# First feed-forward products with tokens in rows, transposed in 32x32 blocks by VectorE and put in place by DMA

## The chip, the cores and the metric

The kernel runs on one NeuronCore of one Trainium2 chip. The metric is the device time of one execution in microseconds (us); lower is better. A core has TensorE (PE, the matrix engine), VectorE (DVE), ScalarE (ACT), GpSimd (POOL), SyncE (SP, which here only issues transfers), and 16 DMA engines. Every engine takes its own instructions strictly in the order in which the program emits them; engines wait for each other by semaphores. On TensorE a matrix product is two instructions: a weight load (PEld, the stationary operand, at most 128x128) and the matmul that streams the moving operand past it into PSUM.

## The reference

Two layers over 256 tokens of width 2048, all in fp32. Each layer has a projection into a conv mixer, an HGRN2 mixer and a retention mixer, an output product, a layer norm, and a feed-forward block with squared ReLU:

```python
for l in range(DEPTH):
    proj = jnp.einsum('btd,de->bte', x, w_in[l])
    ...
    h = jnp.einsum('bte,ed->btd', mix, w_out[l])
    x = layer_norm(DEEPNORM_ALPHA * x + h, ln1_g[l], ln1_b[l]).astype(dtype)
    f = jnp.square(jax.nn.relu(jnp.einsum('btd,df->btf', x, w_ff1[l])))
    h = jnp.einsum('btf,fd->btd', f, w_ff2[l])
    x = layer_norm(DEEPNORM_ALPHA * x + h, ln2_g[l], ln2_b[l]).astype(dtype)
```

`w_ff1` is 2048 x 8192 and `w_ff2` 8192 x 2048. The change concerns the line with `f`: it must end as `f` transposed (columns of `f` on partitions, tokens along the row), since the second product contracts over the columns of `f`.

## The kernel before

**Precision.** TensorE multiplies numbers of a shortened fp32 format (fp32r). Every operand is therefore split into a high part (a rounded copy, made by a cast on ScalarE) and a low part (the rest, a subtraction on VectorE), and each product is the sum of three: high by high, high by low, low by high. For weights this is done in `unit` (L272): 512 KB of a loaded block become one unit, with the cast at L289 and the subtraction at L292. For activations it is `split_act` (L388), cast L391 and subtraction L393.

**Buffers.** Tiles come from rings: three `raw` buffers of 1 MB for loaded weights, six `wp` buffers for split units, eight `act` buffers (each four blocks of 128 contraction rows by 256 tokens, high and low), two `pair` buffers of 128 x 2048, eleven `r2` tiles of 128 x 512, four PSUM tiles `mm` for the large products and four `aux` for the small ones.

**Two forms of product.** `xstat` (L323) makes a group of 512 output columns with the tokens stationary: for each of 16 blocks of contraction and each of two halves of the tokens three matmuls at L315 of 512 columns, 96 in all. Its results are rows: tokens on partitions, columns of the output along the row. `wstat` (L349) makes 256 output columns with the weights stationary and the tokens moving: for each half of 128 columns and each of 16 blocks one matmul of 512 columns (L366: high weights by high and low tokens at once) and one of 256 (L368: low weights by high tokens), 64 in all. Its results are columns: output columns on partitions, tokens along the row. They leave PSUM by a copy on ScalarE (L375) and an addition on VectorE (L378). Both forms load weights by `load2` (L263), 1 MB for two units, issued from SyncE.

**Feed-forward.** For each of four chunks (`for c in range(NCH)`, L1063) four `act` buffers `fT` are filled with 2048 columns of `f`, transposed and split: eight calls of `wstat` (L1077), each followed by ReLU and square in one VectorE operation (L1079) and by `split_act` (L1082). Then four calls of `xstat` with `fT` as the stationary operand (L1099) make this chunk's part of the second product, added to the residual `x_nat` (L963). The very first 512 columns of a layer are an exception: they are made by `xstat` (L1074, so that the tokens whose norm is ready first can be used first: `head=HEAD`), squared in rows (`square_t`, L1066) and turned by TensorE: `transpose4` (L397) makes four 128x128 transposes against an identity matrix, and `split_act` takes them out of PSUM. `w1x` holds these columns' weights, `w1` those of the other 7680.

**Order.** A planner (`Plan`, L71) holds all operations with a cost for each and their dependences through buffers. `run` (L128) goes through them in the order of their planned start on each engine and emits them; among those that can start within 0.12 us it takes the one of least slack. The large products keep the program's order (`main`, L121), the preparation of a unit carries the product that needs it (`needed`, L301), other operations a fixed slack (`slack`, `floor`). Transfers are operations of an engine "DMA" whose results count as seen 2.0 us after their planned end; all of them are issued from SyncE's queue, in planned order. Waits in the running kernel come from the data dependences, whatever the plan assumed.

Of the kernel before, what the change touches and what calls it, by code (L numbers as in the profile page):

```python
# [17 lines left out]
P = 128  # L18
# [182 lines left out]
def block_kernel(ctx: ExitStack, tc: tile.TileContext, a: dict, out: bass.AP):  # L201
# [24 lines left out]
    def act(n, ptr=0, ps=False):  # L226
        return 0.000833 * n + (0.051 if ps else 0.093) + 0.093 * ptr

    def dve(n, ptr=0, fast=False):
        return (0.00052 if fast else 0.001042) * n + 0.069 + 0.06 * ptr  # L230
# [157 lines left out]
    def split_act(x, blks, cols, src, r, part, n=W, ps=False, **kw):  # L388

        nb = blks.stop - blks.start  # L390
        op("ACT", act(n, ps=ps), lambda: S.copy(out=x.t[:, 0, blks, cols], in_=bl(src(), nb)),  # L391
           r=r, w=[(x, part)], **kw)
        op("DVE", dve(n), lambda: V.tensor_tensor(out=x.t[:, 1, blks, cols], in0=bl(src(), nb),  # L393
                                                  in1=x.t[:, 0, blks, cols].bitcast(F32), op=ALU.subtract),
           r=r, w=[(x, part)], **kw)

    def transpose4(src, r, **kw):  # L397
        pt = aux.buf()

        def fn():  # L400
            for i in range(4):
                nc.tensor.transpose(out=pt.t[:, i * P:(i + 1) * P], in_=src()[:, i * P:(i + 1) * P], identity=ident)  # L402

        op("PE", 0.44, fn, r=r, w=[pt], **kw)
        return pt
# [566 lines left out]
        op("DVE", dve(W), fn, r=[ps], w=[(x_nat, (t, c))], **kw)  # L972


    norm = None
    for l in range(DEPTH):
        mixT = [acts.buf() for _ in range(4)]
        vt = []

        def vgroup(g, **kw):  # L980
            tl = []
            vt.append(tl)

            def done(t, ps):
                v = r2.buf()
                op("ACT", act(W, ps=True), lambda: S.copy(out=v.t, in_=ps.t), r=[ps], w=[v], floor=1.5)
                tl.append(v)

            xstat(a["wv"][l, g], xT, done, **kw)

        if l == 0:
            def before(i):
                first_x(i)
                if i == 3:
                    setup((plan.last["PE"],))

            vgroup(0, before=before, fine={0: 4, 2: 2, 4: 2, 6: 2})
            whole(xT[0])
        else:
            vgroup(0, head=HEAD)  # L1000
            norm.rest()
        pairs, gates = {}, {}
        for i, (kind, p) in enumerate(ORDER):
            if (kind, p) == ("hf", 2):
                vgroup(1)
            if (kind, p) == ("rq", 0):
                vgroup(2)
            if kind in ("hf", "rq"):
                pair = pairbufs.buf()
                pairs[kind[0], p] = pair  # L1010
            dst = None
            if kind in ("rq", "rk"):
                dst = (pairs["r", p], "Q" if kind == "rq" else "K", pv(pairs["r", p], 0 if kind == "rq" else 1))
            pr = wstat(a["wp"][l, i], xT, dst)
            if l == 0 and i == 1:
                op("DMA", 6.0, lambda: nc.sync.dma_start(out=x_nat.t, in_=a["x"].rearrange("(t p) d -> p t d", p=P)),
                   w=[x_nat], after=(plan.last["PE"],))
            if kind == "hf":
                hgrn_gates(l, p, pr, pair)
            elif kind == "hq":  # L1020
                Qv = pv(pair, 2)
                op("ACT", act(W), lambda Qv=Qv, pr=pr: S.activation(out=Qv(), in_=pr.t, func=AF.Sigmoid), r=[pr],
                   w=[(pair, "Q")])
                op("DVE", dve(W), lambda Qv=Qv, pr=pr: V.tensor_tensor(out=Qv(), in0=pr.t, in1=Qv(), op=ALU.mult),
                   r=[pr], w=[(pair, "Q")])
            elif kind == "hg":
                gate = r2.buf()
                op("ACT", act(W), lambda gate=gate, pr=pr: S.activation(out=gate.t, in_=pr.t, func=AF.Sigmoid),
                   r=[pr], w=[gate])
                hgrn(l, p, pairs["h", p], gate, vt, mixT)  # L1030
            elif kind in ("cg", "ca"):
                def uv(p=p):
                    return u_t.t[:, 2 * p:2 * p + 2, CONVW - 1:]

                uk = [(u_t, 2 * p), (u_t, 2 * p + 1)]
                if kind == "cg":
                    op("ACT", act(W), lambda uv=uv, pr=pr: S.activation(out=uv(), in_=bl(pr.t, 2), func=AF.Sigmoid),
                       r=[pr], w=uk)
                else:
                    op("DVE", dve(W), lambda uv=uv, pr=pr: V.tensor_tensor(out=uv(), in0=bl(pr.t, 2), in1=uv(),  # L1040
                                                                           op=ALU.mult), r=[pr], w=uk)
                    if p == 0:
                        accs = [r2.buf(), r2.buf()]
                    conv_taps(l, accs[p], 2 * p)
                    if p == 1:
                        conv(l, accs, mixT)
            elif kind == "rg":
                gate = r2.buf()
                op("ACT", act(W), lambda gate=gate, pr=pr: S.activation(out=gate.t, in_=pr.t, func=AF.Sigmoid),
                   r=[pr], w=[gate])  # L1050
                op("DVE", dve(W), lambda gate=gate, pr=pr: V.tensor_tensor(out=gate.t, in0=pr.t, in1=gate.t,
                                                                           op=ALU.mult), r=[pr], w=[gate])
                ret(l, p, pairs["r", p], gate, vt, mixT)
        for g in range(4):
            if g == 1:
                norm = Norm(a["l1g"][l], a["l1b"][l], 2 * l, True)
                norm.add(0, 0, held[0])
                norm.add(0, 1, held[1])
            held = {}
            xstat(a["wo"][l, g], mixT, (lambda t, ps: held.__setitem__(t, ps)) if g == 0 else  # L1060
                  (lambda t, ps: norm.add(g, t, ps)), tail=TAIL if g == 3 else 0)
        xT = norm.xT
        for c in range(NCH):  # L1063
            fT = [acts.buf() for _ in range(4)]

            def square_t(t, ps):  # L1066
                r = r2.buf()
                op("ACT", act(W, ps=True), lambda: S.activation(out=r.t, in_=ps.t, func=AF.Relu), r=[ps], w=[r])
                op("DVE", dve(W), lambda: V.tensor_tensor(out=r.t, in0=r.t, in1=r.t, op=ALU.mult), w=[r])
                pt = transpose4(lambda: r.t, [r, cst])  # L1070
                split_act(fT[0], slice(0, 4), slice(t * P, (t + 1) * P), lambda: pt.t, [pt], t, ps=True)

            if c == 0:
                xstat(a["w1x"][l], xT, square_t, head=HEAD)  # L1074
                norm.rest()
            for q in range(2 if c == 0 else 0, 8):
                r = wstat(a["w1"][l, 8 * c + q - 2], xT)  # L1077
                f = r2.buf()
                op("DVE", dve(W), lambda f=f, r=r: V.scalar_tensor_tensor(  # L1079
                    out=f.t, in0=r.t, scalar=0.0, in1=r.t, op0=ALU.max, op1=ALU.mult), r=[r], w=[f], floor=1.5)  # L1080
                o = (2 * q) % 4
                split_act(fT[q // 2], slice(o, o + 2), slice(0, T), lambda f=f: f.t, [f], ("o", o), floor=1.5)  # L1082
            lastc = c == NCH - 1
            for g in range(4):
                if lastc and g == 1:
                    norm = Norm(a["l2g"][l], a["l2b"][l], 2 * l + 1, False, l == DEPTH - 1)
                    norm.add(0, 0, held[0])
                    norm.add(0, 1, held[1])
                held = {}

                def add(t, ps, g=g, c=c):
                    if lastc and g == 0:
                        held[t] = ps
                    elif lastc:
                        norm.add(g, t, ps)
                    else:
                        residual(g, t, ps, c == 0, floor=1.5)

                xstat(a["w2"][l, c, g], fT, add, tail=TAIL if lastc and g == 3 else 0)  # L1099
        xT = norm.xT  # L1100
# [44 lines left out]
def _xs(w):  # L1145

    k, n = w.shape
    return w.reshape(k // 512, 2, 2, P, n // W, W)\
        .transpose(4, 0, 3, 1, 2, 5).reshape(n // W, k // 512, P, 2048)


def _ws(w):

    k, n = w.shape
    return w.reshape(2, 8, P, n // 256, 2, P).transpose(3, 4, 2, 0, 1, 5).reshape(n // 256, 2, P, 2048)
# [52 lines left out]
```

## Time and profile before

| | us |
|---|---|
| median of 3 runs | 2325.21 |
| lowest and highest run | 2323.97, 2325.35 |
| the profiled execution, its own time | 2324.98 |
| its span, first to last instruction | 2323.1 |

The profile shows one execution. "Busy" is the time in which an engine executes; waits, branches and the issuing of transfers don't count. The page's second part cuts the span into 40 slices, one digit for each (9 is 90% or more):

```profile
PE   9999999999999999999999999999999999999998
DVE  6999666765565565565679986657655655655655
ACT  6445444454344344344444554544444444444442
DMA  8544556465555555556554545564655555555563
```

The repeated patterns are the two layers. DMA moves

```profile
DMA packets 67706, 439.90 MB, mean 189 GB/s; under 512 B 7665, under 2 KB 7921, under 8 KB 16625
```

in the whole span. Five kinds of views are used below: the page; groups of instructions by source line, with count, total and mean duration, and the idle time ahead of them with what ended it; the chain of work that ended last, followed back from the last instruction; sums by windows of time; and the waits, who waited for whom, SyncE's queue (SPq) among them. Of a line's or a tile's own instructions a further view gives least, median and longest duration. Windows are given in us from the start of the span.

### The profile page before, as it was taken

How to read it: one execution, taken by the hardware profiler on the slowest of the kernel's cores; microseconds unless marked ns; L12 is line 12 of the kernel's file. 1: busy time of each engine (PE TensorE's matmuls, PEld its weight loads, DVE VectorE, ACT ScalarE, POOL GpSimd, SP SyncE). 2: the span in 40 equal slices, each digit the busy share in tenths (PEclk: the TensorE clock that was granted, in tenths of full speed). 3: DMA queues.
4: the chain of work that ended last, by engine and by line, in shares of the span. 5: the costliest groups of instructions: out<-in, count | busy, mean ns of one | idle time of the engine just before them, and what ended most of it. 6: DMA issues, size and time to landing. Idle time of an engine off the chain costs nothing.

```text
span 2323.1 us, 29492 instructions
## 1 busy us (share of the span) xinstructions
PE 2308.4 (99%) x11995; PEld 1961.7 (84%) x11995; DVE 1512.1 (65%) x2077; ACT 1055.0 (45%) x1346; POOL 47.1 (2%) x60
## 2 busy tenths in 40 slices
PE   9999999999999999999999999999999999999998
PEld 7888888888888888888888888888888888888886
DVE  6999666765565565565679986657655655655655
ACT  6445444454344344344444554544444444444442
POOL 0001000000000000000000000100000000000000
PEclk9999999999999999999999999999999999999999
DMA  8544556465555555556554545564655555555563
GB/s 297 186 166 164 174 195 209 165 211 195 193 188 185 196 184 197 188 189 203 209 173 164 175 165 179 179 227 166 205 192 189 185 196 189 192 185 196 183 232 112
DMA packets 67706, 439.90 MB, mean 189 GB/s; under 512 B 7665, under 2 KB 7921, under 8 KB 16625
## 3 DMA queue, kind: packets, MB, share of 16 engines
q1 hardware_dynamic: 67568, 438.01, 55.1%
q8 instruction: 94, 1.54, 0.3%
q14 instruction: 44, 0.35, 0.0%
HBM read 432.74 MB, written 2.10 MB: 187 GB/s over the span
## 4 chain that ended last, share of the span: by engine, by line
PE 98%; DMA 1%; ACT 1%; DVE 1%; issue 0%; SPq 0%; DVEq 0%; ACTq 0%
PE mm L315 44%; PE mm L366 34%; PE mm L368 17%; PE aux L634 1%; PE aux L402 1%; DMA raw<-in_wv 0%; ACT act L391 0%; DMA raw<-in_xt 0%; DVE wp L292 0%; PE aux L556 0%; PE aux L558 0%; PE aux L554 0%; PE aux L747 0%; ACT wp L289 0%; PE aux L610 0%; ACT r L943 0%
## 5 line engine op out<-in xcount | busy, mean ns | idle before, releaser
L292 DVE TENSOR_TENSOR wp<-raw,wp 128x1024 fp32r<-128x1024 f32 (+1 forms) x786 | 957.5, 1221 | 573.7 <-ACT wp L289 572.6
L366 PE MATMUL mm<-act,wp 128*128 128x512 f32 x3328 | 1180.3, 399 | 0.0
L289 ACT CAST wp<-raw 128x1024 fp32r<-128x1024 f32 (+1 forms) x786 | 824.8, 1052 | 770.9 <-PE mm L315 503.5
L315 PE MATMUL mm<-wp,act 128*128 128x512 f32 x4416 | 1017.8, 390 | 3.3 <-DVE wp L292 2.0
L315 PEld LDWEIGHTS mm<-wp,act 128*128 128x128 f32 x4416 | 824.5, 188 | 178.3 <-DVE wp L292 5.9
L368 PE MATMUL mm<-act,wp 128*128 128x256 f32 x3328 | 933.4, 280 | 0.0
L366 PEld LDWEIGHTS mm<-act,wp 128*128 128x128 f32 x3328 | 625.4, 188 | 151.9
L368 PEld LDWEIGHTS mm<-act,wp 128*128 128x128 f32 x3328 | 628.4, 189 | 0.7
L375 ACT COPY r<-mm 128x256 f32<-128x256 f32 x208 | 77.5, 373 | 368.2 <-PE mm L368 367.9
L378 DVE TENSOR_TENSOR r<-mm,r 128x256 f32<-128x256 f32 x184 | 78.0, 424 | 142.9 <-ACT r L375 142.2
L821 DVE SCALAR_TENSOR_TENSOR r<-u_t,cst,r 128x256 f32<-128x256 f32 x240 | 103.9, 480 | 0.0
L410 POOL TENSOR_TENSOR sm<-sm,mhalf 128x4 f32<-128x4 f32 (+1 forms) x24 | 28.6, 1193 | 2266.5 <-DVE sm L903 1611.8
L391 ACT CAST act<-r 128x512 fp32r<-128x512 f32 x82 | 51.4, 630 | 17.0 <-DVE r L1079 16.1
L393 DVE TENSOR_TENSOR act<-r,act 128x512 fp32r<-128x512 f32 x82 | 56.2, 685 | 0.0
L315 PE MATMUL mm<-act,act 128*128 128x512 f32 x192 | 44.8, 389 | 0.0
L970 DVE TENSOR_TENSOR x_nat<-x_nat,mm 128x512 f32<-128x512 f32 x48 | 31.1, 682 | 18.8 <-PE mm L315 18.7
L1079 DVE SCALAR_TENSOR_TENSOR r<-r 128x512 f32<-128x512 f32 x60 | 41.6, 693 | 2.1
L315 PEld LDWEIGHTS mm<-act,act 128*128 128x128 f32 x192 | 36.0, 188 | 7.5
L634 PEld LDWEIGHTS aux<-pair 128*126 128x126 f32 (+5 forms) x288 | 31.3, 173 | 3.9 <-DVE r L821 1.2
L634 PE MATMUL aux<-pair 128*126 128x64 f32 (+5 forms) x288 | 31.9, 253 | 0.0
L968 DVE SCALAR_TENSOR_TENSOR x_nat<-x_nat,mm 128x512 f32<-128x512 f32 x32 | 20.8, 682 | 13.1 <-PE mm L315 13.0
L923 ACT ACTIVATE x_nat<-x_nat,sm 128x512 f32<-128x512 f32 x6 | 4.9, 817 | 48.1 <-POOL sm L416 48.1
(123 smaller groups left out, 591.5 us busy)
## 6 DMA issues: line engine op xcount, KB each, us to landing
raw<-in_w SPq DMA_DIRECT2D x248, 1024.0 KB, 4.8
raw<-in_wp SPq DMA_DIRECT2D x88, 1024.0 KB, 4.8
raw<-in_wo SPq DMA_DIRECT2D x32, 1024.0 KB, 4.8
raw<-in_wv SPq DMA_DIRECT2D x20, 1024.0 KB, 4.8
raw<-in_w1x SPq DMA_DIRECT2D x8, 1024.0 KB, 5.2
raw<-in_wv SPq DMA_DIRECT2D x6, 512.0 KB, 6.0
pair<-pair SPq DMA_DIRECT2D x24, 128.0 KB, 2.3
x_nat<-in_x SPq DMA_DIRECT2D x1, 2048.0 KB, 9.4
```

Source lines behind the costliest of these rows:

```text
L289: S.copy(out=wt()[:, 0, sl], in_=raw.t[:, rs])
L292: V.tensor_tensor(out=wt()[:, 1, sl], in0=raw.t[:, rs], in1=wt()[:, 0, sl].bitcast(F32), op=ALU.subtract)
L315: nc.tensor.matmul(ps.t, lhsT=xT[k // 4].t[:, xs, k % 4, t * P:(t + 1) * P], rhs=w[:, ws, kb, :], start=(k == 0 and n == 0), stop=(k == KB ...
L366: nc.tensor.matmul(pv, lhsT=w[:, 0, kb, :], rhs=xt[:, :, k % 4, :], start=(k == 0), stop=False)
L368: nc.tensor.matmul(pv[:, 0, :], lhsT=w[:, 1, kb, :], rhs=xt[:, 0, k % 4, :], start=False, stop=(k == KB - 1))
L375: S.copy(out=low.t, in_=ps.t[:, T:])
L378: V.tensor_tensor(out=dst[2]()[:, b * T:(b + 1) * T], in0=ps.t[:, 0:T], in1=low.t, op=ALU.add)
L391: op("ACT", act(n, ps=ps), lambda: S.copy(out=x.t[:, 0, blks, cols], in_=bl(src(), nb)), r=r, w=[(x, part)], **kw)
L393: op("DVE", dve(n), lambda: V.tensor_tensor(out=x.t[:, 1, blks, cols], in0=bl(src(), nb), in1=x.t[:, 0, blks, cols].bitcast(F32), op=ALU.s ...
L634: nc.tensor.matmul(ps.t[0:P - L, b * 64:(b + 1) * 64], lhsT=Kt()[:, b * P:(b + 1) * P - L], rhs=rhs, start=True, stop=True)
L821: V.scalar_tensor_tensor(out=d, in0=src, scalar=cw[:, l, b, j:j + 1], in1=d, op0=ALU.mult, op1=ALU.add)
L1079: op("DVE", dve(W), lambda f=f, r=r: V.scalar_tensor_tensor(out=f.t, in0=r.t, scalar=0.0, in1=r.t, op0=ALU.max, op1=ALU.mult), r=[r], w=[f ...
```

## The change

Fifteen of the sixteen groups of 512 columns of the first product are made by `xstat`; the sixteenth, the last of the last chunk, stays with `wstat`. The arrays `w1x` and `w1` are cut accordingly. What leaves `xstat` goes through a new function `hidden`:

- ReLU out of PSUM on ScalarE and square on VectorE, for each half `t` of the tokens, in rows;
- `V.transpose`, which transposes each 32x32 block in place of its grid, written into the first half of a `pair` buffer;
- 16 transfers from SyncE, four to a planner operation with a cost of 1.7 us: the transfer (i, j) takes the blocks of partition group i and column group j to partition group j and column group i, in the second half of the same buffer. Each has 32 partitions and four runs of 64 fp32 (256 B);
- the copy that makes the high part in `fT` on ScalarE and the subtraction that makes the low part on VectorE, for each half of the tokens.

TensorE's transposes of the first group (`square_t`) go. The buffers `fT` of all four chunks are declared ahead of the loop, and each chunk makes the first group of the next chunk before its own second product: groups 0 to 4, then 5 to 8, 9 to 12, and 13 to 15.

```diff
+    def hidden(product, w, xT, fT, **kw):
+        fb = pairbufs.buf()
+
+        def quarters(half, p0, n):
+            return fb.t[p0:p0 + n, half * 1024:(half + 1) * 1024].rearrange("p (k j t e) -> p k j t e", k=4, j=4, t=2)
+
+        def done(t, ps):
+            r = r2.buf()
+            op("ACT", act(W, ps=True), lambda: S.activation(out=r.t, in_=ps.t, func=AF.Relu), r=[ps], w=[r], floor=1.5)
+            op("DVE", dve(W), lambda: V.tensor_tensor(out=r.t, in0=r.t, in1=r.t, op=ALU.mult), w=[r])
+            op("DVE", dve(W), lambda: V.transpose(out=quarters(0, 0, P)[:, :, :, t, :], in_=r.t.rearrange(
+                "p (k j e) -> p k j e", k=4, j=4)), r=[r], w=[(fb, ("s", t))])
+
+        product(w, xT, done, **kw)
+        for i in range(4):
+            def move(i=i):
+                for j in range(4):
+                    nc.sync.dma_start(out=quarters(1, 32 * j, 32)[:, :, i], in_=quarters(0, 32 * i, 32)[:, :, j])
+
+            op("DMA", 1.7, move, r=[(fb, ("s", 0)), (fb, ("s", 1))], w=[(fb, ("f", i))])
+        rk = [(fb, ("f", i)) for i in range(4)]
+        for t in range(2):
+            cols = slice(t * P, (t + 1) * P)
+
+            def part(s, cols=cols):
+                return fT.t[:, s, :, cols].rearrange("p k (i e) -> p k i e", i=4)
+
+            def src(t=t):
+                return quarters(1, 0, P)[:, :, :, t, :]
+
+            op("ACT", act(W), lambda part=part, src=src: S.copy(out=part(0), in_=src()), r=rk, w=[(fT, t)])
+            op("DVE", dve(W), lambda part=part, src=src: V.tensor_tensor(
+                out=part(1), in0=src(), in1=part(0).bitcast(F32), op=ALU.subtract), r=rk, w=[(fT, t)])
...
+        fTs = [[acts.buf() for _ in range(4)] for _ in range(NCH)]
         for c in range(NCH):
-            fT = [acts.buf() for _ in range(4)]
-
-            def square_t(t, ps):
-                r = r2.buf()
-                op("ACT", act(W, ps=True), lambda: S.activation(out=r.t, in_=ps.t, func=AF.Relu), r=[ps], w=[r])
-                op("DVE", dve(W), lambda: V.tensor_tensor(out=r.t, in0=r.t, in1=r.t, op=ALU.mult), w=[r])
-                pt = transpose4(lambda: r.t, [r, cst])
-                split_act(fT[0], slice(0, 4), slice(t * P, (t + 1) * P), lambda: pt.t, [pt], t, ps=True)
-
-            if c == 0:
-                xstat(a["w1x"][l], xT, square_t, head=HEAD)
-                norm.rest()
-            for q in range(2 if c == 0 else 0, 8):
-                r = wstat(a["w1"][l, 8 * c + q - 2], xT)
...
+            fT = fTs[c]
+
+            for n in range(4 * c + min(c, 1), min(4 * c + 5, 16)):
+                if n < 15:
+                    hidden(xstat, a["w1x"][l, n], xT, fTs[n // 4][n % 4], head=0 if n else HEAD)
+                    if n == 0:
+                        norm.rest()
+                    continue
+                for q in range(2):
+                    r = wstat(a["w1"][l, q], xT)
...
-    a["w1x"] = np.stack([_xs(i["w_ff1"][l][:, :W])[0] for l in range(DEPTH)])
-    a["w1"] = np.stack([_ws(i["w_ff1"][l][:, W:]) for l in range(DEPTH)])
+    a["w1x"] = np.stack([_xs(i["w_ff1"][l][:, :15 * W]) for l in range(DEPTH)])
+    a["w1"] = np.stack([_ws(i["w_ff1"][l][:, 15 * W:]) for l in range(DEPTH)])
```

More of the change, by code (lines that the diff above doesn't have):

```diff
@@ L1062, in block_kernel @@
         xT = norm.xT
+        fTs = [[acts.buf() for _ in range(4)] for _ in range(NCH)]
         for c in range(NCH):
-            fT = [acts.buf() for _ in range(4)]
-            def square_t(t, ps):
-                r = r2.buf()
-                op("ACT", act(W, ps=True), lambda: S.activation(out=r.t, in_=ps.t, func=AF.Relu), r=[ps], w=[r])
-                op("DVE", dve(W), lambda: V.tensor_tensor(out=r.t, in0=r.t, in1=r.t, op=ALU.mult), w=[r])
-                pt = transpose4(lambda: r.t, [r, cst])
-                split_act(fT[0], slice(0, 4), slice(t * P, (t + 1) * P), lambda: pt.t, [pt], t, ps=True)
-            if c == 0:
-                xstat(a["w1x"][l], xT, square_t, head=HEAD)
-                norm.rest()
-            for q in range(2 if c == 0 else 0, 8):
-                r = wstat(a["w1"][l, 8 * c + q - 2], xT)
[L1078 to L1082, printed above, removed]
+            fT = fTs[c]
[7 more added lines that the diff above has]
+                    r = wstat(a["w1"][l, q], xT)
+                    f = r2.buf()
+                    op("DVE", dve(W), lambda f=f, r=r: V.scalar_tensor_tensor(
+                        out=f.t, in0=r.t, scalar=0.0, in1=r.t, op0=ALU.max, op1=ALU.mult), r=[r], w=[f], floor=1.5)
+                    split_act(fT[3], slice(2 * q, 2 * q + 2), slice(0, T), lambda f=f: f.t, [f], ("o", 2 * q),
+                              floor=1.5)
             lastc = c == NCH - 1
```

## The prediction

> **What bounds the kernel now.** I read the page first: the busy times, then the chain that ended last.
>
> ```profile
> span 2323.1 us, 29492 instructions
> PE 2308.4 (99%) x11995; PEld 1961.7 (84%) x11995; DVE 1512.1 (65%) x2077; ACT 1055.0 (45%) x1346; POOL 47.1 (2%) x60
> PE 98%; DMA 1%; ACT 1%; DVE 1%; issue 0%; SPq 0%; DVEq 0%; ACTq 0%
> ```
>
> TensorE is busy for 99% of the span and holds 98% of the chain, so time can only leave through TensorE's own work, and it can only be added by making TensorE wait. The question is therefore what one group of 512 feed-forward columns costs TensorE in the old form (weights stationary, columns out, L366 and L368) and in the new one (tokens stationary, rows out, L315). The chain in order of time cuts the feed-forward of layer 0 into stages; the windows view over these stages (length of the stretch, busy time and instruction starts of each engine, granted clock, DMA share) prices them:
>
> ```profile
> core 0: us, PE busy (x) PEld busy (x) DVE busy (x) ACT busy (x) POOL busy (x), PEclk, DMA share, GB/s
> 540.37:627.42 87.05, 87.05 (x386) 72.07 (x385) 44.78 (x42) 34.63 (x34) 0.00 (x0) 1.00 0.58 194
> 627.42:717.86 90.44, 90.44 (x514) 78.39 (x513) 54.84 (x63) 42.04 (x54) 0.00 (x0) 1.00 0.54 186
> 717.86:804.92 87.06, 87.06 (x386) 72.07 (x385) 44.78 (x42) 34.63 (x34) 0.00 (x0) 1.00 0.57 193
> 804.92:895.37 90.45, 90.45 (x514) 78.48 (x513) 54.85 (x63) 42.05 (x54) 0.00 (x0) 1.00 0.55 187
> 895.37:982.43 87.06, 87.06 (x385) 72.07 (x385) 44.78 (x42) 34.63 (x34) 0.00 (x0) 1.00 0.57 193
> 982.43:1072.88 90.45, 90.45 (x514) 78.40 (x513) 54.84 (x63) 42.04 (x54) 0.00 (x0) 1.00 0.54 186
> ```
>
> Stretches of 87.05 us are second products (`w_ff2`), four row groups of 96 matmuls: 21.76 us a group, 226.7 ns a matmul. Stretches of 90.45 us are first products, eight calls of `wstat`, which make four groups of 512 columns with 128 matmuls each (half of 512 columns, half of 256): 22.61 us a group, 353 ns a pair. TensorE has no gap in either, and the granted clock is 1.00 in both. Both forms stream the same number of columns; the old one is cut into a third more instructions and pays 0.85 us a group for it. The row form's pace is no property of the second product, since the `w_out` stage, with other operands, has it too (84.33/372 = 226.7 ns):
>
> ```profile
> 358.84 84.33 PE mm L315 x372
> ```
>
> **The change part by part.**
>
> *TensorE, removed.* Per layer 15 of 16 groups are now in rows; one was before, so 14 change form. Two layers: 28 × (22.61 − 21.76) = 28 × 0.847 = 23.7 us. The group that was in rows already also loses its TensorE transposes, four calls of four, which the chain shows one by one:
>
> ```profile
> 468.93 0.44 PE aux L402 x4
> 474.93 0.44 PE aux L402 x4
> ...
> 1621.86 0.44 PE aux L402 x4
> 1627.85 0.44 PE aux L402 x4
> ```
>
> That is 4 × 0.44 = 1.8 us. Together 25.5 us of TensorE work goes, and nothing is added on it.
>
> *VectorE and ScalarE.* These run beside TensorE, so the question is only whether they still fit.
>
> ```profile
> L292 DVE TENSOR_TENSOR wp<-raw,wp 128x1024 fp32r<-128x1024 f32 (+1 forms) x786 | 957.5, 1221 | 573.7 <-ACT wp L289 572.6
> L289 ACT CAST wp<-raw 128x1024 fp32r<-128x1024 f32 (+1 forms) x786 | 824.8, 1052 | 770.9 <-PE mm L315 503.5
> L391 ACT CAST act<-r 128x512 fp32r<-128x512 f32 x82 | 51.4, 630 | 17.0 <-DVE r L1079 16.1
> L393 DVE TENSOR_TENSOR act<-r,act 128x512 fp32r<-128x512 f32 x82 | 56.2, 685 | 0.0
> L1069 DVE TENSOR_TENSOR r<-r 128x512 f32<-128x512 f32 x4 | 2.7, 685 | 0.0
> L1068 ACT ACTIVATE r<-mm 128x512 f32<-128x512 f32 x4 | 2.4, 598 | 1.2 <-PE mm L315 1.2
> ```
>
> A group in rows has eight weight units in either form. VectorE: 8 × 1.22 for the units, 2 × 0.685 for the squares, 2 × 0.685 for the low halves, and two transposes. No row shows a VectorE transpose. From below it is a 512-element pass (0.685), from above two 1024-element passes (2.44); I take 0.69, the row with its size. Sum 13.9 us, at the upper end 17.4, against 54.84/4 = 13.7 now and 21.76 available. ScalarE: 8 × 1.05 + 2 × 0.598 + 2 × 0.630 = 10.9 us, against 42.04/4 = 10.5. If the strided reads of the final copies doubled those two, it would be 12.2. All fit; cost on the path nothing. [...]
>
> *The DMAs.* This is what the trace of before shows least: 16 moves a group, each 32 partitions by four runs of 256 B (32 KB). They cost SyncE's time to issue, DMA engine time, and a latency in front of the copies.
>
> ```profile
> L717 SPq DMA_DIRECT2D pair<-pair x12: 467/467/531, 260.4 to 1487.0; - x12
> L718 SPq DMA_DIRECT2D pair<-pair x12: 584/590/1336, 261.0 to 1487.5; - x12
> L266 SPq DMA_DIRECT2D raw<-in_w x248: 327/328/896, 431.9 to 2282.6; - x124
> pair<-pair SPq DMA_DIRECT2D x24, 128.0 KB, 2.3
> raw<-in_w SPq DMA_DIRECT2D x16, 1024.0 KB, 4.8
> 2316.00:2323.10 7.10, 0.00 (x0) 0.00 (x0) 4.10 (x7) 0.00 (x0) 0.84 (x1) 0.50 0.39 148
> ```
>
> The first three rows give min/median/max issue time in ns, the fourth and fifth us to landing (the fifth in the window 627.42 to 717.86, so four loads a group). *Issue:* the nearest rows, copies within the same buffers, take 0.47 and 0.59 us; 16 × 0.53 + 4 × 0.33 = 9.8 us of SyncE a group; from 6.5 (all at the load's 0.33) to 22.7 (all at the longest copy, 1.336). *Engines:* the last row is the output, four stores of 128 rows of 2 KB: 0.39 × 7.1 × 16 / 512 = 87 ns a row. A run of 256 B lies between an eighth of that (11 ns) and all of it; I take 20 ns, near the end that goes by bytes. 2048 runs on 16 engines make 2.6 us a group, 1.4 to 11.1; the loads take 0.54 × 22.61 = 12.2, the sum is 14.8, at most 23.3 of 21.76. *Latency:* 16 issues, a landing of 2.3 us and one wait behind a load that still wants its buffer (5.5 us at the longest, next fence): 9 + 2 + 5 = some 16 us from the transposes to the last landing.
>
> [...]
>
> *What the moves can hold up.* A move waits on SyncE for the transposes, and the next weight load waits behind it; the ScalarE copy into `fT` waits for the moves, and the weight casts wait behind that copy. So a late move reaches TensorE only through weights. Their lead:
>
> ```profile
> ACT wp L289 <- PE mm L315: 50.5, 31, 1.7
> SPq L266 <- DVE wp L292: 84.0, 16, 5.5
> ```
>
> In the window 540.37 to 627.42, 31 of 32 casts waited for TensorE to give a weight buffer back: the six buffers are full, five units ahead, 5 × 2.7 = 13.6 us less a cast and a subtraction, say 11 us. In the window 627.42 to 717.86 each of the 16 loads waited for a raw buffer, so SyncE idles too. A stall of ScalarE or SyncE below 11 us a group costs nothing, and per group ScalarE regains 11, VectorE 8 us.
>
> *The order.* The result of a group is wanted late: group 4 of 0 to 15 (the one ahead) stands between group 3 and the second product, which reads group 3's buffer last, at three quarters of its first group, 21.8 + 16.3 = 38 us after group 3 ends. Squares, transposes, moves, copies take about 0.6 + 0.7 + 0.7 + 16 + 1.3 = 19 us. Without the ahead group 16.3 us would be too little. In the last chunk the old-form group (22.6 us) and half a group stand behind group 14: 33 us. The ahead group holds no `fT` buffer during the second product (eight are in use) but its `pair` buffer; the copy runs when `fT` comes free in the last of the four, a chunk before it is needed. Cost nothing.
>
> **Sum.** The profiled run took 2324.98 us, its span 2323.1 and 1.9 around it; the median of the runs is 2325.21, 0.2 above. 2324.98 − 23.7 − 1.8 = 2299.5, with the median's offset 2299.7; I say **2299.6**, 1.1% less. A measurement here can tell about 0.2% (4.6 us) from no change.
>
> **The rivals.**
>
> A. *Part of the gain is given back* (chance 0.12). After each norm TensorE starts with an empty weight lead, and the order of all queues is planned anew. Half a microsecond of waiting in each of the 30 groups returns 15 us: 2314 to 2316. For it: 1 to 5 us of latency on SyncE is not in the trace. Against it: the 11 us lead.
>
> B. *The form is not what costs* (0.07). If the 0.85 us belonged to the stage (its evictions, which share PSUM with TensorE), it would stay, and only the transposes go: 2324.98 − 1.8 = 2323.2, no measurable change. Against it: the row form has 226.7 ns in two stages, and no stage of L366 and L368 shows a gap. [...]
>
> C. *The moves go one at a time* (0.13), slower. They write interleaved columns of one buffer half; if each had to wait on SyncE for the landing of the one before, a move would hold the queue for 0.53 + 2.3 = 2.8 us, 16 of them 45 us, while the loads behind need 21.76. The point from which it decides: 30 groups × excess, less a lead of 11 us in each of eight chunks, must reach 25.5 us; excess 3.8 us, that is (21.76 + 3.8 − 1.3)/16 = 1.5 us a move. At 2.8 us, 30 × (45 + 1.3 − 21.8) − 88 = +650, some 2950 us. At the longest issue time of the rows, 1.34, nothing. For it: the trace has no such interleaved writes. Against it: L718 is issued straight after L717 though both write one buffer (other partitions). If only moves into the same partitions wait, there are four rounds of 2.8 us, 11 us, which changes nothing. [...]
>
> **How the numbers follow.** Forecast 0.68, A 0.12, B 0.07, C 0.13. The forecast's own range is 2295 to 2304 (the pace to 0.05 us a group, 1.5 us, and a few us for the new order of layer 1). Forecast and A together hold 0.80: 2294 to 2316. The upper ends of the unknown costs (transposes 17.4 us, engines 23.3, issue 22.7) exceed a group by at most 1.6 us, 6 us a chunk, inside the lead, so they need no wider range. Faster 0.80, same 0.07, slower 0.13.
>
> **What would show it.** Right: L366 and L368 fall from 3328 to 1536 each, L315 grows by 2688; four-group stretches of the first product last 87.06 us, the last chunk's two row groups and one old 66.1; L402 loses 16; SyncE's issues of `pair<-pair` rise by 480 at about 0.5 us; VectorE's transposes take 0.69 us; ScalarE's copies wait for the moves a few us a group, TensorE for no weight. Wrong: TensorE waiting on L289 or L292 in the first products (A, C); SyncE waiting on `pair<-pair` before each move, or over 1.5 us a move (C); first products still 22.6 us a group (B).

## The result and the profile after

The changed kernel takes 2299.36 us (median of 4 runs, 2297.87 to 2299.71) against 2324.59 for the kernel before beside it: ratio 0.9888, 95% interval 0.9876 to 0.9901, 25.2 us less in the medians. 2299.6 was forecast.

The page of the changed kernel, its span, busy times and chain by engine:

```profile
span 2297.9 us, 28385 instructions
PE 2283.4 (99%) x11083; PEld 1917.4 (83%) x11083; DVE 1497.6 (65%) x2025; ACT 1044.5 (45%) x1290; POOL 48.0 (2%) x60
PE 98%; ACT 1%; DVE 1%; DMA 0%; issue 0%; SPq 0%; DVEq 0%
```

TensorE is as full as before and has 912 matmuls less: 14 x 2 groups with 32 fewer, and 16 transposes. Its busy time fell by 25.0 us, the span by 25.2. Nothing else moved the end.

The chain in order of time, at the feed-forward of layer 0:

```profile
461.88 575.39 PE mm L315 x2537
```

From inside the first group to the end of the fifteenth TensorE runs without a single foreign piece, through three second products: 575.39/2537 = 226.8 ns a matmul. The windows of two stages in it, a second product and then the first product behind it (columns as in the prediction):

```profile
558.27:645.36 87.09, 87.09 (x386) 72.15 (x385) 49.73 (x49) 38.01 (x40) 0.00 (x0) 1.00 0.66 228
645.36:732.45 87.09, 87.09 (x386) 72.13 (x385) 47.15 (x48) 36.77 (x42) 0.00 (x0) 1.00 0.57 183
```

Four groups of either product now take 87.09 us, where a first product took 90.45. The new groups of instructions, and the moves by their issues (ns: least, median, longest) and landing (us):

```profile
L988 DVE STREAM_TRANSPOSE pair<-r 128x512 f32<-128x512 f32 x60 | 42.5, 708 | 1.1
L1008 ACT CAST act<-pair 128x512 fp32r<-128x512 f32 x60 | 34.9, 619 | 75.5 <-DMA pair<-pair 70.6
L1009 DVE TENSOR_TENSOR act<-pair,act 128x512 fp32r<-128x512 f32 x60 | 39.3, 688 | 57.6 <-ACT act L1008 57.4
L995 SPq DMA_DIRECT2D pair<-pair x480: 585/599/1663, 473.9 to 2192.1; - x160
pair<-pair SPq DMA_DIRECT2D x480, 32.0 KB, 1.9
```

The transposes cost about what a pass of 512 elements costs (708 ns against 685), and the strided reads cost the copies nothing (619 and 688 ns against 630 and 685 for L391 and L393 before). ScalarE does wait for the moves, 70.6 us in all, and TensorE does not notice. One group's way, from three views of the timeline (start, length, engine, line, output and input, count, idle time before it and its releaser): ScalarE, SyncE and VectorE,

```profile
884.96 1.07 ACT L986 ACTIVATE r<-mm 128x512 f32<-128x512 f32 x2
...
901.75 1.14 ACT L1008 CAST act<-pair 128x512 fp32r<-128x512 f32 x2 [2.10 <-DMA pair<-pair]
```

```profile
890.02 10.37 SPq L995 DMA_DIRECT2D pair<-pair  x16
```

```profile
902.40 1.29 DVE L1009 TENSOR_TENSOR act<-pair,act 128x512 fp32r<-128x512 f32 x2 [1.50 <-ACT act L1008]
```

from ReLU at 884.96 to the low halves at 903.69: 18.7 us, more than half of it the 16 issues.

### The profile page after: what moved, and what is told of

Read it like the earlier page. It is cut to its first block, busy times and chain, and to the rows that moved or that the text cites. A ratio compares the mean times of both kernels' runs of the same rounds, so it can differ in the third digit from the quotient of the medians.

```text
span 2297.9 us, 28385 instructions
## 1 busy us (share of the span) xinstructions
PE 2283.4 (99%) x11083; PEld 1917.4 (83%) x11083; DVE 1497.6 (65%) x2025; ACT 1044.5 (45%) x1290; POOL 48.0 (2%) x60
## 4 chain that ended last, share of the span: by engine, by line
PE 98%; ACT 1%; DVE 1%; DMA 0%; issue 0%; SPq 0%; DVEq 0%
PE mm L315 71%; PE mm L366 16%; PE mm L368 8%; PE aux L634 1%; PE aux L402 1%; DMA raw<-in_wv 0%; DVE wp L292 0%; PE aux L556 0%; ACT act L391 0%; PE aux L558 0%; PE aux L554 0%; PE aux L747 0%; ACT wp L289 0%; PE aux L610 0%; ACT r L943 0%; PE aux L677 0%
## 5 line engine op out<-in xcount | busy, mean ns | idle before, releaser
L315 PE MATMUL mm<-wp,act 128*128 128x512 f32 x7104 | 1625.7, 390 | 2.9 <-ACT wp L289 1.6
L315 PEld LDWEIGHTS mm<-wp,act 128*128 128x128 f32 x7104 | 1331.4, 188 | 281.1 <-DVE wp L292 3.6
L366 PE MATMUL mm<-act,wp 128*128 128x512 f32 x1536 | 546.4, 399 | 0.0
L368 PE MATMUL mm<-act,wp 128*128 128x256 f32 x1536 | 430.1, 280 | 0.0
L366 PEld LDWEIGHTS mm<-act,wp 128*128 128x128 f32 x1536 | 288.7, 188 | 67.7
L368 PEld LDWEIGHTS mm<-act,wp 128*128 128x128 f32 x1536 | 290.0, 189 | 0.5
L375 ACT COPY r<-mm 128x256 f32<-128x256 f32 x96 | 35.9, 374 | 156.9 <-PE mm L368 156.5
L1009 DVE TENSOR_TENSOR act<-pair,act 128x512 fp32r<-128x512 f32 x60 | 39.3, 688 | 57.6 <-ACT act L1008 57.4
L1008 ACT CAST act<-pair 128x512 fp32r<-128x512 f32 x60 | 34.9, 619 | 75.5 <-DMA pair<-pair 70.6
L378 DVE TENSOR_TENSOR r<-mm,r 128x256 f32<-128x256 f32 x72 | 30.4, 422 | 32.7 <-ACT r L375 32.3
L988 DVE STREAM_TRANSPOSE pair<-r 128x512 f32<-128x512 f32 x60 | 42.5, 708 | 1.1
L987 DVE TENSOR_TENSOR r<-r 128x512 f32<-128x512 f32 x60 | 40.1, 668 | 0.0
L986 ACT ACTIVATE r<-mm 128x512 f32<-128x512 f32 x60 | 34.2, 594 | 12.6 <-PE mm L315 12.6
```

Source lines behind the costliest of these rows:

```text
L315: nc.tensor.matmul(ps.t, lhsT=xT[k // 4].t[:, xs, k % 4, t * P:(t + 1) * P], rhs=w[:, ws, kb, :], start=(k == 0 and n == 0), stop=(k == KB ...
L366: nc.tensor.matmul(pv, lhsT=w[:, 0, kb, :], rhs=xt[:, :, k % 4, :], start=(k == 0), stop=False)
L368: nc.tensor.matmul(pv[:, 0, :], lhsT=w[:, 1, kb, :], rhs=xt[:, 0, k % 4, :], start=False, stop=(k == KB - 1))
L375: S.copy(out=low.t, in_=ps.t[:, T:])
L988: op("DVE", dve(W), lambda: V.transpose(out=quarters(0, 0, P)[:, :, :, t, :], in_=r.t.rearrange("p (k j e) -> p k j e", k=4, j=4)), r=[r], ...
L1008: op("ACT", act(W), lambda part=part, src=src: S.copy(out=part(0), in_=src()), r=rk, w=[(fT, t)])
```

## The experiments

The theory: TensorE's own work decides, the row form saves 0.85 us a group, and everything that was added is hidden. The first four runs take this apart, the seventh asks what the 0.85 us is made of, the others how far the hiding reaches. The medians, with the kernel before as it ran beside each:

| kernel | us | ratio to before | 95% interval |
|---|---|---|---|
| rows, turned by TensorE | 2325.74 | 1.0003 | 0.9993 to 1.0012 |
| no group ahead | 2325.58 | 1.0000 | 0.9990 to 1.0011 |
| all sixteen groups in rows | 2304.60 | 0.9911 | 0.9896 to 0.9926 |
| no moves | 2299.18 | 0.9887 | 0.9870 to 0.9903 |
| 32 moves | 2553.05 | 1.0982 | 1.0966 to 1.0999 |
| 48 moves | 2866.80 | 1.2333 | 1.2313 to 1.2354 |
| before, long low matmuls | 2661.16 | 1.1447 | 1.1430 to 1.1464 |
| 24 moves | 2398.67 | 1.0324 | 1.0307 to 1.0341 |
| 24 moves, planned at 3.9 us | 2377.34 | 1.0221 | 1.0206 to 1.0236 |
| 32 moves, planned at 5.2 us | 2501.49 | 1.0761 | 1.0745 to 1.0777 |
| 16 moves, planned at 2.6 us | 2299.52 | 0.9892 | 0.9877 to 0.9907 |
| all in rows, two queues | 2298.71 | 0.9886 | 0.9869 to 0.9902 |

### The form alone

```diff
-    hidden(xstat, a["w1x"][l, n], xT, fTs[n // 4][n % 4], head=0 if n else HEAD)
+    turned(a["w1x"][l, n], xT, fTs[n // 4][n % 4], head=0 if n else HEAD)
-for n in range(4 * c + min(c, 1), min(4 * c + 5, 16)):
+for n in range(4 * c, 4 * c + 4):
```

`turned` is `xstat` with the `square_t` of the kernel before.

> The same fifteen groups in rows, but turned by TensorE (four 128x128 transposes for each half of the tokens, as the first group was before), no VectorE transposes, no moves, no group ahead. Theory (TensorE's own work decides, the form gives 0.85 us a group): 30 groups x 8 transposes x 0.11 us = 26.4 us come back on top of the changed kernel's 2299.4, so about 2325.8, no measurable change against before; the first products' groups last 21.77 + 0.88 = 22.65 us each. Rival (the 0.85 us belongs to the stage and the gain came from somewhere else): the row form itself saves nothing, so the transposes cost on top of before, 28 x 0.88 = 24.6 us, about 2350. Rival (the moves cost hidden time in the changed kernel): below 2320.

2325.74 us. Its chain in order of time:

```profile
495.47 0.87 PE aux L402 x8
496.35 21.81 PE mm L315 x96
518.15 0.87 PE aux L402 x8
519.03 21.78 PE mm L315 x96
```

A group takes 21.79 us and its transposes 0.87, together what the column form took. So the form does save its 0.85 us, and turning the result on TensorE spends just that. The gain needs both parts of the change: the form, and a way to turn the result that costs TensorE nothing.

### The moves alone

```diff
-        for i in range(4):
-            def move(i=i):
...
-        rk = [(fb, ("f", i)) for i in range(4)]
+        rk = [(fb, ("s", 0)), (fb, ("s", 1))]
...
-                return quarters(1, 0, P)[:, :, :, t, :]
+                return quarters(0, 0, P)[:, :, :, t, :]
```

> The changed kernel without its 480 moves: the copies read the blocks where VectorE left them, so the blocks of f stay in the wrong places. Theory (the moves are wholly hidden): 2299.4, within 2 us, while SyncE loses 480 issues and the DMA share of the first products falls by a tenth. Rival (the moves take time from the path, by contention with the weight loads or by ScalarE waiting): the time falls by what they take, up to 70 us, which is what ScalarE's copies waited for them in total in the changed kernel.

This kernel leaves out the 480 moves. It takes 2299.18 us, the changed kernel's time within 0.2 us, so the moves and ScalarE's waits for them cost nothing there. The DMA queue's row of the page (packets, MB, share of 16 engines), first of this kernel, then of the changed one:

```profile
q1 hardware_dynamic: 67568, 438.01, 55.9%
```

```profile
q1 hardware_dynamic: 136688, 453.77, 58.2%
```

480 moves take 2.3% of the engines' time, 0.023 x 2297.9 x 16 = 846 us, 14 ns for each of the 61440 runs of 256 B. The rows differ by 69120 packets, 16 a move more than its 128 runs, and the time of these is in it.

### The group ahead

```diff
-for n in range(4 * c + min(c, 1), min(4 * c + 5, 16)):
+for n in range(4 * c, 4 * c + 4):
```

> The changed kernel with the groups in order, 0 to 3, 4 to 7, 8 to 11, 12 to 15: no group ahead of a chunk. Theory (a group's way from PSUM into fT takes about 19 us in the trace of the changed kernel, 884.9 to 903.9, and the second product wants it 16.3 us after the group ends): TensorE waits 2 to 3 us at three chunks of each layer, 6 x 2.2 = 13 us, about 2312, with the waits at three quarters of the first group of the second product, for the low halves in fT. Rival (the order hides nothing, the planner or the engines take up the 2 us): 2299.4.

2325.58 us: the whole gain is gone, twice what was expected. The waits (total, times, longest) and TensorE's busy time:

```profile
PE mm L315 <- ACT act L1008: 16.7, 6, 5.8
```

```profile
PE 2292.4 (99%) x11083; PEld 1921.1 (83%) x11083; DVE 1500.1 (65%) x2025; ACT 1046.2 (45%) x1290; POOL 47.1 (2%) x60
```

Six waits for `fT`, as expected in number and place (though it is the copy of the high halves that comes last, not the low halves), make 16.7 us: 3.94, 1.28 and 1.50 us in layer 0, 5.83, 2.08 and 2.12 us in layer 1. Another 9.0 us are in TensorE's busy time (2292.4 against 2283.4 for the same matmuls). TensorE's timeline at the first wait, and windows behind the waits of 3.94, 1.28, 5.83 and 2.12 us:

```profile
555.92 19.42 PE L315 MATMUL mm<-wp,act 128*128 128x512 f32 x76 [3.94 <-ACT act L1008]
```

```profile
555.90:560.00 4.10, 4.08 (x10) 3.01 (x11) 2.52 (x3) 1.43 (x2) 0.00 (x0) 0.60 0.94 382
733.50:735.50 2.00, 2.00 (x8) 1.35 (x9) 1.82 (x3) 1.39 (x2) 0.00 (x0) 1.00 0.89 373
1707.70:1709.70 2.00, 1.96 (x5) 1.53 (x6) 1.81 (x3) 1.46 (x2) 0.00 (x0) 0.50 0.96 381
2065.40:2067.40 2.00, 1.98 (x5) 1.56 (x6) 1.82 (x3) 1.44 (x2) 0.00 (x0) 0.50 0.97 385
```

After 3.94 us of waiting the granted clock is 0.60 for some 4 us, another 1.6 us lost. It falls in the same way after 5.83, 2.08 and 2.12 us, to 0.50, and is whole again within 4 to 8 us of the restart; after 1.28 and 1.50 us it stays at 1.00. What the clock lacked in these windows and the ones behind them adds up to 8.2 of the 9.0 us.

The first wait is 2.7 us longer than the second. From the group's ReLU (L986) to TensorE's restart both take 17.5 us, so the difference lies ahead of the ReLU, in ScalarE's queue. Its timeline, for the first wait and then for the second:

```profile
533.68 1.15 ACT L1008 CAST act<-pair 128x512 fp32r<-128x512 f32 x2 [5.08 <-DMA pair<-pair]
538.44 1.08 ACT L986 ACTIVATE r<-mm 128x512 f32<-128x512 f32 x2
...
711.56 1.14 ACT L1008 CAST act<-pair 128x512 fp32r<-128x512 f32 x2 [2.76 <-DMA pair<-pair]
716.02 1.08 ACT L986 ACTIVATE r<-mm 128x512 f32<-128x512 f32 x2
```

Before the first wait ScalarE stood 5.08 us for the moves of the group before, against 2.76 us before the second, and so came to the ReLU that much later.

### The sixteenth group

```diff
-                if n < 15:
+                if n < 16:
```

with `w1x` for all columns and `w1` left out.

> The changed kernel with the sixteenth group in rows too. Theory: two more groups change form, 2 x 0.85 = 1.7 us less on TensorE, but nothing stands any more between the last group and the second product of the last chunk, so that TensorE waits 2 to 3 us there in each layer; together 2299.4 - 1.7 + 4 to 6 = 2302 to 2304. Rival (the way into fT is short enough or is taken up): 2297.7.

2304.60 us, 5.2 above the changed kernel. Its waits have

```profile
PE mm L315 <- ACT act L1008: 3.4, 2, 2.6
```

two waits, 0.80 us in layer 0 and 2.61 in layer 1. The profiled span is 3.4 us longer, as much as the waits. The 1.7 us expected from the form don't show in TensorE's busy time (2283.6 against 2283.4), because the clock took them back: it stays at 1.00 after the wait of 0.80 us and falls after that of 2.61.

```profile
2220.00:2222.00 2.00, 2.00 (x6) 1.57 (x5) 0.74 (x1) 0.00 (x0) 0.00 (x0) 0.50 1.04 438
```

With the windows of 2 us on either side of this one (0.76 and 0.89) the clock lost 1.7 us. The rest of the 5.2 us lies between this profiled execution (2303.10, the fastest of four) and the median; the profile does not place it.

### What the 0.85 us is made of

```diff
-    nc.tensor.matmul(pv[:, 0, :], lhsT=w[:, 1, kb, :], rhs=xt[:, 0, k % 4, :],
+    nc.tensor.matmul(pv, lhsT=w[:, 1, kb, :], rhs=xt[:, :, k % 4, :],
```

> The kernel before, with the low weights in the column form multiplied by high and low activations (512 columns instead of 256, so the low by low product is computed in addition). It asks what the 0.85 us a group is made of. Theory 1 (each matmul pays the same 13.4 ns over its stream, and a 256-column one some 6.6 ns more, because the next weight load is not hidden behind it): a pair of two 512-column matmuls takes 2 x 226.7 = 453.4 ns, 3328 pairs x (453.4 - 353.3) = 333 us, about 2658. Theory 2 (the pair's extra belongs to the column form, whatever the length): 353.3 + 106.7 = 460.0 ns a pair, + 355 us, about 2680.

2661.16 us, 336.1 above the kernel before beside it (2325.1): 101.0 ns for each of 3328 pairs, so that a pair of long matmuls takes 454.3 ns, two at 227.2. Theory 1 (453.4 ns) holds against theory 2 (460.0): the column form pays for nothing but its instructions. A matmul of 512 columns costs some 227 ns in either form; one of 256 costs 353.3 - 226.7 = 126.6 ns, more than half. By that a group costs 64 x 353.3 ns = 22.6 us in the column form (128 matmuls) and 96 x 226.7 ns = 21.8 us in the row form. Whether the short matmul's excess is a fixed cost of each matmul or a weight load that the shorter stream does not cover, as theory 1 has it, this run does not tell.

### How far the moves stay hidden

```diff
-nc.sync.dma_start(out=quarters(1, 32 * j, 32)[:, :, i], in_=quarters(0, 32 * i, 32)[:, :, j])
+for ks in (slice(0, 2), slice(2, 4)):
+    nc.sync.dma_start(out=quarters(1, 32 * j, 32)[:, ks, i], in_=quarters(0, 32 * i, 32)[:, ks, j])
```

and, for 48, slices of one, one and two blocks. The bytes are the same, only the issues grow.

> The changed kernel with each move cut in two (two runs of 256 B a partition each), 32 issues a group. Theory (a move is harmless until it holds SyncE for about 1.5 us, the point worked out in the prediction): two issues at 0.6 us make 1.2 us a move, 19.2 + 1.3 us a group, just under a group's 21.77; but the way into fT grows by 9.6 us to about 29 us, under the 38 us that the group ahead gives, and under the 33 us of the last chunk; 2299 to 2304. Rival (the weight lead is thinner than 11 us, or loads behind moves come late): 2310 to 2400, with TensorE waiting for casts and subtractions of weights in the first products.

> The changed kernel with each move cut in three, 48 issues a group. Theory: 48 x 0.6 + 1.3 = 30.1 us of SyncE a group, 8.4 us over a group; by the prediction's formula 30 x 8.4 - 88 = 164 us come on top of 2299.4, about 2460, with TensorE waiting for weights and SyncE issuing moves without a pause in the first products. The way into fT is about 39 us, which adds some us at chunks. Rival (issue time does not hold up the weights, since loads slip in between): within 10 us of 2299.4. Rival (issue falls with fewer runs a transfer, toward 0.33 us): 48 x 0.4 = 19 us, also about 2300.

2553.05 and 2866.80 us: both expectations failed. In the profile of 32 moves:

```profile
ACT act L1009 <- DMA pair<-pair: 365.1, 24, 18.6
PE mm L315 <- ACT wp L289: 176.3, 25, 9.0
```

TensorE starves for weight casts, and ScalarE stands before its copy. Two theories followed, one that the copy's place in ScalarE's queue decides, one that SyncE's throughput does, and a kernel between the two:

```diff
+for ks in (slice(0, 2), slice(2, 4)) if j < 2 else (slice(0, 4),):
```

> The changed kernel with half of its moves cut in two, 24 issues a group, the planner's cost left at 1.7 us for each of the four blocks of moves. Theory S (what decides is the place of ScalarE's copy in its own queue: with 16 moves a block of 10.3 us on SyncE and waits of 2 to 6 us, with 32 a block of 20.5 us, waits of 16.4 us, of which TensorE feels 8): block 15.4 us, the copy waits some 11 us, TensorE 3 us in each of 30 groups, about 2390. Theory Q (SyncE's throughput decides, once issues fill a group): 24 x 0.64 + 1.3 = 16.7 of 21.77 us, no loss, 2299 to 2302.

2398.67 us, near theory S's 2390, but not by its sum: TensorE waits for casts 16 times, not in each of 30 groups, 49.8 us in all. The page's busy times:

```profile
PE 2320.6 (97%) x11083; PEld 1931.7 (81%) x11083; DVE 1489.1 (62%) x2025; ACT 1035.0 (43%) x1290; POOL 48.0 (2%) x60
```

TensorE's are 37.2 us more than the changed kernel's for the same matmuls, at a mean granted clock of 0.985 against 0.998. So over a third of the loss is a slower TensorE behind its waits, as in the run with no group ahead. One group in SyncE's, ScalarE's and TensorE's timelines:

```profile
743.65 16.36 SPq L996 DMA_DIRECT2D pair<-pair  x24
760.11 12.08 SPq L266 DMA_DIRECT2D raw<-in_w  x4
```

```profile
748.41 1.05 ACT L289 CAST wp<-raw 128x1024 fp32r<-128x1024 f32 x1 [2.19 <-DMA raw<-in_w]
761.37 1.14 ACT L1009 CAST act<-pair 128x512 fp32r<-128x512 f32 x2 [11.90 <-DMA pair<-pair]
762.41 1.04 ACT L289 CAST wp<-raw 128x1024 fp32r<-128x1024 f32 x1
766.48 1.04 ACT L289 CAST wp<-raw 128x1024 fp32r<-128x1024 f32 x1 [3.03 <-DMA raw<-in_w]
```

```profile
763.50 0.49 PE L315 MATMUL mm<-wp,act 128*128 128x512 f32 x1 [4.04 <-ACT wp L289]
```

While SyncE issues 24 moves in one block, no load goes out; ScalarE makes its last cast at 748.41, stands at the copy for 11.9 us, and TensorE runs dry at 759.46. The units ready at 750.7 (that cast and its subtraction done) lasted 8.8 us, not the 11 of the prediction. One landed unit stood behind the copy in ScalarE's queue; the next (766.48) had to wait for a load that SyncE issued after the moves. Then the planner was told what a block takes:

```diff
-op("DMA", 1.7, move, r=[(fb, ("s", 0)), (fb, ("s", 1))], w=[(fb, ("f", i))])
+op("DMA", 3.9, move, r=[(fb, ("s", 0)), (fb, ("s", 1))], w=[(fb, ("f", i))])
```

for 24 moves, 5.2 us for 32 and 2.6 us for 16.

> As the kernel with 24 moves, but the planner is told what a block of them takes, 3.9 us in place of 1.7, so that the copies are emitted later and weight casts ahead of them; work and transfers are the same. Theory S: ScalarE's waits for moves fall to a few us and TensorE waits for no weight, 2299 to 2303. Theory Q: the same time as with 24 moves and the cost of 1.7.

> 32 moves a group as in the run with each move cut in two (2553), the planner told 5.2 us a block in place of 1.7. Theory S: most of the loss goes, but SyncE is now almost full (20.5 + 1.3 of 21.77 us), and the way into fT of some 35 us meets the 38 and 33 us that the order gives: 2300 to 2330. Theory Q: about 2550 as before.

> The changed kernel as it is, the planner told 2.6 us a block of moves in place of 1.7 (16 issues of 0.64 us are 10.3 us). Theory S: ScalarE's waits for moves, 71 us in total and 6.3 us at the longest, shrink; the time does not change, 2299.4, since TensorE does not feel them.

2377.34, 2501.49 and 2299.52 us. The waits of TensorE, with 24 moves planned at 1.7 us and then at 3.9:

```profile
PE mm L315 <- ACT wp L289: 49.8, 16, 4.9
```

```profile
PE mm L315 <- ACT act L1009: 55.2, 10, 13.2
PE mm L315 <- ACT wp L289: 1.1, 1, 1.1
```

SyncE's timeline with the planner told:

```profile
723.36 3.79 SPq L996 DMA_DIRECT2D pair<-pair  x6
727.24 0.54 SPq L266 DMA_DIRECT2D raw<-in_w1x  x1
```

The block is broken up, loads go out between, and TensorE's waits for weights all but go: the order that the planner made is the cause of the first wait, not SyncE's throughput (theory Q). Whether it is the copy's place in ScalarE's queue, as theory S has it, or the loads' place in SyncE's is not told apart, since the edit moves both. The expected time missed all the same, for a second wait took its place: with loads between, the moves end later, and the copy comes too late for the second product. With 32 moves at 5.2 us it is the same, with 170.7 us of such waits. So more issues cost time either way, once the cover is used up. With the 16 moves of the changed kernel, told the truth (2.6 us), ScalarE's waits fall and the time stays, as expected; before and after that edit:

```profile
ACT act L1008 <- DMA pair<-pair: 70.6, 24, 6.3
```

```profile
ACT act L1008 <- DMA pair<-pair: 19.0, 6, 3.9
```

### A version with all sixteen groups

```diff
-                    nc.sync.dma_start(out=quarters(1, 32 * j, 32)[:, :, i], in_=quarters(0, 32 * i, 32)[:, :, j])
+                    q = nc.scalar if both and j % 2 else nc.sync
+                    q.dma_start(out=quarters(1, 32 * j, 32)[:, :, i], in_=quarters(0, 32 * i, 32)[:, :, j])
```

with `both` for the last group alone.

> The kernel with all sixteen groups in rows (2304.6), with half of the last group's moves issued from ScalarE's queue, so that eight issues of 0.64 us stand one after another in place of sixteen. Theory: the last group's way into fT falls from about 19 to 14 us, below the 16.3 us after which the second product wants it; the waits of 2.6 and 0.8 us and the drop of the clock behind them go, and two groups more have the cheaper form: 2299.4 - 1.7 = 2297.7, hardly below the changed kernel. Rival (the ScalarE issues hold up its casts there): 2300 to 2305.

2298.71 us: 5.9 below all sixteen groups from one queue, so the last group's way into `fT` was most or all of what these had lost. Of the two waits one is left, 1.54 us in layer 1, and the clock behind it stays at 1.00. The time is not told apart from the changed kernel's (2299.36; the intervals of the two ratios overlap).

## Why the prediction was right, and where its working was not

The forecast was 25.5 us of TensorE work gone and nothing added on the path, and that is what came: 25.0 us gone and nothing added. That forecast and median agree to 0.2 us is luck, since the kernel before ran 0.6 us faster beside the changed one (2324.59) than where the forecast started from (2325.21). Point by point:

- **TensorE.** A group was to fall from 22.61 to 21.76 us; it took 87.09/4 = 21.77. Busy time fell by 25.0 us, and the turned version (2325.74, expected 2325.8) shows that the gain is the form's. Rival B, that the form is not what costs, is out; the long low matmuls show the cost to be that of each instruction, 227.2 ns for one of 512 columns in the column form as against 226.8 in rows, and 126.6 ns for one of 256. No run shows the 13.4, 6.6 and 106.7 ns that the two theories of that run name; what it shows in place of the 106.7 is 101.0 ns more for a pair whose short matmul is made 256 columns longer.
- **VectorE and ScalarE.** A transpose was put at 0.69 us and took 0.708; the copies 0.619 and 0.688 against 0.630 and 0.685. Right.
- **DMA engines.** 20 ns a run were taken, 14 measured, nearer to the 11 ns that go by bytes.
- **Issue and latency.** 0.53 us an issue was too low (0.60, 0.64 with the gap), 2.3 us landing too high (1.9). That the way of 19 us came out (18.7) is luck, by the group shown: ReLU to the first move took 5.1 us where 2.0 stood, since both halves of the tokens and a weight subtraction come one after another; the moves took 11.7 us where 16 stood, since the 5 us behind a load did not come. The copies wait for the moves, and nobody waits for that: rival A did not come, and without the moves the time is the same.
- **The order.** That 16.3 us would be too little without the group ahead was right, and worth more than the step said: 26.2 us, of which 16.7 are waits and some 8 the clock behind them, a cost that neither the prediction nor the expectation had.
- **The steps that failed**, without touching the forecast, are "A stall of ScalarE or SyncE below 11 us a group costs nothing" and, built on it in rival C, the point of "1.5 us a move". The lead was counted as full when the stall begins, and SyncE's and ScalarE's stalls as if each came alone. They come together, out of one block of moves, and last to the moment when the copy is done.
- **Where the point lies instead.** Measured: 16 issues 2299.4, 24 issues 2398.7, 32 issues 2553.1, 48 issues 2866.8. From 24 to 32 that is 154.4 us, 5.1 a group, for 8 x 0.64 = 5.1 us of issues, so past its point a microsecond of issue costs about one of time. Part of it is the clock: TensorE's busy time grew by 29.0 us from 24 to 32, the rest of the span by 126.7 us, 4.2 a group. Drawn back from 24 at one for one, the point lies near 19 issues by the time (99.3/30 = 3.3 us, five issues) and near 21 by the span without TensorE's busy time (61.1/30 = 2.0 us, three issues): a block of 12 to 13 us, or some 0.8 us a move, an estimate from these runs, none of which has between 16 and 24. The changed kernel, with 10.3, is 2 to 3 us short of it, where the prediction saw a factor of more than two. The margin that it gave itself against rival C was not there; that the moves are not made to wait for each other's landing (16 issues in 10.37 us, 1.9 us to landing) is what kept C away.

That the sixteenth group in rows lost 5.2 us in the median where the profile accounts for 3.4 stays open, and so does what makes a matmul of 256 columns cost more than half of one of 512.

## What to carry to other kernels

On a kernel that TensorE fills, count what each form of a product issues, not only what it streams: a quarter fewer matmuls for the same columns were worth 3.7% of that product, and would have been worth nothing had TensorE turned the result. Work that is moved off the full engine is free only while a queue that also feeds that engine stays short of its cover (here it was free with 16 issues a group and cost 99.3 us with 24); find the cover's end by adding issues, since the profile before shows only that there is one. When a result gets a longer way, put other work of the full engine between it and its use, and look for the clock as well as the wait where that work is missing (here 16.7 us of waits and some 8 us of clock).

## What the runs showed of the hardware that was not expected

The issue time of a move hardly changed with its size: 599, 595 and 592 ns in the median with 32 KB, 16 KB and 8 to 16 KB a move, so cutting each move in two doubled SyncE's time for a group, from 10.37 to 20.95 us in the groups shown by the timelines of the two kernels. With no group ahead and with all sixteen groups in rows, waits of 2.08, 2.12, 2.61, 3.94 and 5.83 us brought the granted clock down to about half for some microseconds, while waits of 0.80, 1.28 and 1.50 us left it at 1.00. The length of a wait alone does not decide, since with 24 moves one of 2.24 us (ended at 607.83) left it at 1.00 too. In the run with 48 moves a group the mean granted clock was 0.910 against 0.998. In the changed kernel a move was held up on SyncE by VectorE's transposes 30 times, and 15 times, by the profile's account, by a weight load:

```profile
SPq L995 <- DVE pair L988: 17.2, 30, 3.3
SPq L995 <- DMA raw<-in_w1x: 3.3, 8, 1.5
SPq L995 <- DMA raw<-in_w: 3.0, 7, 1.1
```

though a move needs nothing of what those loads bring. The profile infers who released a wait, and no run shows what such a load holds up.
